# Weight splits ranked 400 instructions earlier, and the second head pair of a gated linear attention projected beside head 1 instead of head 0

## The chip, the cores and the metric

The kernel runs on one core of a Trainium2 chip. The metric is device time in microseconds (us) of one execution. The engines are TensorE (PE in the profile; PEld is its weight load), VectorE (DVE), ScalarE (ACT), GpSimd (POOL) and SyncE (SP), which starts most of the transfers.

## What is computed

512 tokens of width 1024, and 256 context tokens, go through two blocks of two layers each, all in float32. The change acts in the first block. A layer projects the normalised tokens to all inputs of three branches and three gates, and merges the branches:

```python
hx = rms_norm(xs, norm_g) * (1 + scale_x[:, None]) + shift_x[:, None]
px = split_cols(hx @ w_in + b_in)
...
ya_x = conv_module(*px[0:3], dw_w, dw_b, ln_g, ln_b, w_conv_out)
yb_x, yb_c = gla_branch(px[3:9], pc[3:9], gla_w_gate, gla_b_gate, gla_norm_g, w_gla_out, need_ctx)
yc_x, yc_c = attn_branch(px[9:13], pc[9:13], q_norm_g, k_norm_g, w_attn_out, need_ctx)
...
return (jax.nn.sigmoid(p[13]) * ya + jax.nn.sigmoid(p[14]) * yb
        + jax.nn.sigmoid(p[15]) * yc) @ w_out
```

The branch in question is the gated linear attention (GLA): four heads with keys of 64 and values of 128, scanned forward and backward in chunks of 64 tokens, the context first. Per chunk, with `cum` the running sum of the log gate:

```python
q_in = q * jnp.exp(cum)
k_in = k * jnp.exp(-cum)
att = jnp.where(mask, jnp.einsum('bnihd,bnjhd->bnhij', q_in, k_in), 0.0)
o_intra = jnp.einsum('bnhij,bnjhe->bnihe', att, v)
k_state = k * jnp.exp(last[:, :, None] - cum)
contrib = jnp.einsum('bnjhd,bnjhe->bnhde', k_state, v)
...
return dec[..., None] * s + con, s
```

The first layer needs the context's outputs too (768 tokens), the second only those of the 512. The second block (mLSTM and retention) is not touched by name, but uses the same function for its weights.

## The kernel before

All large products are made from pairs: each float32 operand is split into a rounded high part and the rest, and `mm3` (L317) issues three products, high with high, high with low and low with high. Weights come from HBM in granules of 128x1024 or 128x512: `raw` (L270, a transfer started by SP) brings one into a buffer wr, and `split` makes wh from it (L285, ScalarE, a rounded copy) and wl (L286, VectorE, the difference). wr, wh and wl have two buffers each, so that a granule can be split when TensorE has finished with the last but one.

The program is written in Python generators that are woven into each other. What each engine then does in which order is set by a scheduler: of the instructions that are ready by its model, it takes the one with the best rank, and the rank is the order of issue in the program. `high_priority(offset=400)` ranks what is issued under it as if it had come 400 instructions sooner.

In the first block the projections use PSUM tiles `pp` (three banks of 512 columns), and the GLA heads tiles `pm`. The generators of GLA:

- `gla_in`: values, and the queries and keys of heads 0 and 1 through `gla_qk(0)`.
- `gla_qk(hp)`: the queries (here Q1 for hp 1) and then the keys (K1) of heads 2hp and 2hp+1. After each projection the pieces in `pp` are emptied by ScalarE, each half of a piece twice (L935, L936), into tiles bq0 or bk0 for the even head, which have one buffer, and bq1 or bk1 for the odd head, which have two. In layer 0 such a projection is 768 columns, two `pp` tiles of 512 and 256.
- `gla_gate(hd)`: the log gate of a head from L948 on, its running sums (two scans, L956 and L958), the scaled queries and keys (L972, L977, L978), and the keys transposed on TensorE (L984).
- `gla_body(hd, go)`: contributions (L998), 22 state updates (L1008), the masked scores (L1019, L1021, L1025), the head's outputs (L1029, L1033, which reads bq), and their norm (`per_token`, L625 to L641, `rsqrt` L302 to L308, L1040, L1041).
- `gla_`: drives them, with a generator `ahead` that is advanced between the steps of a head's body.

`gla_` is woven with `merge`, which projects the merge gates (granules M00 to M07, copied from PSUM by L763, used by L775) and the conv branch's output (w_conv_out 0 to 7). These products don't depend on GLA and fill TensorE beside it. Attention follows: per two query tiles the scores (L1234), softmax (reduce L1237, exponential L1239, L1240, scaling L1241), transposes (L1254) and the products with the values (L1264), woven with the later gates and the output projections.

Of the kernel before, what the change touches and what calls it, by code (L numbers as in the profile page):

```python
# [9 lines left out]
F32 = mybir.dt.float32  # L10
# [4 lines left out]
AF = mybir.ActivationFunctionType  # L15
ALU = mybir.AluOpType
# [243 lines left out]
class _K:  # L260
# [12 lines left out]
    def split(self, spec, spare=None):  # L273

        nk, nc_ = spec[3], spec[5]
        n = nk * nc_
        r = self.raw(spec)[:, :n]
        if spare is None:
            hi = self.wh.tile([P, 1024], F32R, tag="wh", name="wh")[:, :n]
            lo = self.wh.tile([P, 1024], F32R, tag="wl", name="wl")[:, :n]  # L280
        else:
            c = slice(TX + P * spare, TX + P * spare + n // KT)
            hi, lo = self.hh[:, :, c], self.hl[:, :, c]
            r = r.rearrange("p (k c) -> p k c", k=KT)
        self.nc.scalar.activation(hi, r, AF.Copy)  # L285
        self.nc.vector.tensor_tensor(out=lo, in0=r, in1=hi.bitcast(F32), op=ALU.subtract)  # L286
        return hi, lo

    @staticmethod
# [282 lines left out]
def _chain(*gens):  # L572
    for g in gens:
        yield from g


def _first_block(K, ctx, resp):
# [10 lines left out]
    def layer(l, res, t3p, ctx2, pend):  # L588
        need = l < DEPTH - 1
# [20 lines left out]
        def vec(name, i=0, p0=0, p1=P, half=False):  # L610
            c = _S1[name] + i - (h0 if half else g0)
            return (smh if half else sm)[p0:p1, c:c + 1]
# [115 lines left out]
        def tin(c, segs):  # L728
            return K.proj_t(("w_in", l, 0, 8, c, 128), h, segs)
# [151 lines left out]
        with tc.tile_pool(name="gla", bufs=1) as gp, tc.tile_pool(name="glaps", bufs=8 - K.pp_banks, space=PSUM) as pm:  # L881
# [45 lines left out]
            def gla_qk(hp):  # L927
                for name, col, segs in (("bq", C_Q, outs), ("bk", C_K, full)):
                    pcs = tin(col + 128 * hp, segs)
                    for i in range(2):  # L930
                        t = gp.tile([P, 768], F32, tag=f"{name}{i}", name=name, bufs=1 + i)
                        b_ = vec(name, 2 * hp + i, 64 * i, 64 * i + 64)
                        for ps, s, e in pcs:
                            src = ps[64 * i:64 * i + 64, :]
                            S.activation(t[0:64, s:e], src, AF.Identity, bias=b_)  # L935
                            S.activation(t[64:128, s:e], src, AF.Identity, bias=b_)  # L936
                        qk[name, 2 * hp + i] = t
                    yield
# [118 lines left out]
            def gla_():  # L1057

                yield from gla_gate(0)
                for hd in range(4):  # L1060
                    ahead = _chain(gla_gate(1), gla_qk(1)) if hd == 0 else gla_gate(hd + 1) if hd < 3 else iter(())
                    for i, _ in enumerate(gla_body(hd, go)):
                        if i % 2 == 0 or not need or hd == 0:
                            next(ahead, None)
                        yield
                    for _ in ahead:
                        pass
            gla = gla_()
            n_gla, n0 = (43, 3) if need else (27, 3)
            n_tap = 37 if need else 34  # L1070
# [735 lines left out]
```

## Time and profile before

| | |
|---|---|
| median of 3 runs (range) | 2748.11 us (2747.8 to 2751.84) |
| the profiled execution | 2749.59 us |
| its span | 2747.5 us |
| mean granted TensorE clock | 0.977 of full |
| TensorE busy | 2609.0 us, 95% |
| VectorE busy | 1984.6 us, 72% |
| ScalarE busy | 1089.8 us, 40% |
| chain that ended last, by engine | PE 79%, DVE 15%, ACT 3% |

The trace has one row for each instruction, with its engine, source line, output and input. "Idle before <- releaser" is the time that the engine stood ahead of it, and whose end released it. A wait for several things is put down to the last. PEclk is the TensorE clock that was granted, as a share of 2.4 GHz; its lower level is 1.2 GHz. The first block ends at about 1600 us; layer 0 of it has its GLA heads at about 220 to 370 us, layer 1 at about 1085 to 1235.

### The profile page before, as it was taken

The page shows a single profiled execution, that of the slowest core. Times are in us where ns is not written, and L with a number is a line of the kernel's source. Part 1 is how long each engine was busy: PE and PEld are TensorE (multiplying, and loading weights), DVE is VectorE, ACT ScalarE, POOL GpSimd, SP SyncE. Part 2 cuts the span into 40 slices and gives each one's busy share as a digit, 9 for nine tenths or more (in the row PEclk, how much of TensorE's full clock was granted, in tenths as well). Part 3 has the DMA queues.
Part 4 walks back from the last instruction along what each step waited for, and adds up shares of the span by engine and source line. Part 5 has one row for each costly group of instructions (what it writes and reads, how often), then busy time and mean ns, then how long its engine had stood idle before and what let it go on. Part 6 is the DMA issues. An engine that isn't in the chain of part 4 may idle for free.

```text
span 2747.5 us, 37004 instructions
## 1 busy us (share of the span) xinstructions
PE 2609.0 (95%) x14484; PEld 2222.0 (81%) x14484; DVE 1984.6 (72%) x3691; ACT 1089.8 (40%) x1819; POOL 27.8 (1%) x94
## 2 busy tenths in 40 slices
PE   5998899999899999699999989999999999999998
PEld 3887778888788788578877878888888978888887
DVE  5998565677875599766888678776677678655665
ACT  3234423454532334534545344442333444432332
POOL 0000000000000000000000000000000000000000
PEclk9999999999999999899999999999999999999999
DMA  5210103101253231013134424334332222223222
GB/s 210 64 56 29 39 28 103 55 30 62 71 156 100 88 97 62 27 61 112 58 111 130 139 80 137 121 117 130 123 123 77 82 82 83 84 80 92 77 85 77
DMA packets 78110, 243.18 MB, mean 89 GB/s; under 512 B 9968, under 2 KB 16496, under 8 KB 77808
## 3 DMA queue, kind: packets, MB, share of 16 engines
q1 hardware_dynamic: 72448, 233.37, 27.2%
q10 hardware_dynamic: 5488, 7.44, 0.9%
q8 instruction: 114, 1.87, 0.3%
q14 instruction: 60, 0.49, 0.1%
HBM read 238.68 MB, written 2.10 MB: 88 GB/s over the span
## 4 chain that ended last, share of the span: by engine, by line
PE 79%; DVE 15%; ACT 3%; issue 2%; DMA 1%; ACTq 0%; POOL 0%; DVEq 0%
PE pp L317 63%; PE pm L317 5%; DVE ca L814 4%; PE ov L1264 2%; DVE wl L286 2%; PE sc L1234 2%; DVE SP L1008 2%; PE tr L1254 2%; ACT wh L285 1%; PE pm L1033 1%; PE pm L635 1%; PE pm L625 1%; DVE t L958 1%; PE pm L1685 1%; DVE t L956 0%
## 5 line engine op out<-in xcount | busy, mean ns | idle before, releaser
L317 PE MATMUL pp<-hh,wh 128*128 128x512 f32 (+1 forms) x2080 | 772.5, 373 | 35.1 <-ACT bk L936 12.4
L317 PE MATMUL pp<-hh,wl 128*128 128x512 f32 (+1 forms) x2080 | 768.0, 372 | 28.8 <-DVE wl L286 28.7
L317 PE MATMUL pp<-hl,wh 128*128 128x512 f32 (+1 forms) x2080 | 767.9, 371 | 1.4 <-DVE hl L472 1.3
L285 ACT ACTIVATE wh<-wr 128x1024 fp32r<-128x1024 f32 (+1 forms) x348 | 347.6, 1000 | 769.1 <-PE pp L317 696.8
L286 DVE TENSOR_TENSOR wl<-wr,wh 128x1024 fp32r<-128x1024 f32 (+1 forms) x348 | 399.2, 1148 | 195.5 <-ACT wh L285 190.4
L317 PEld LDWEIGHTS pp<-hh,wh 128*128 128x128 f32 x2080 | 396.6, 191 | 103.2 <-ACT bk L936 13.1
L317 PEld LDWEIGHTS pp<-hh,wl 128*128 128x128 f32 x2080 | 396.4, 191 | 100.7 <-DVE wl L286 36.4
L317 PEld LDWEIGHTS pp<-hl,wh 128*128 128x128 f32 x2080 | 396.9, 191 | 64.8 <-DVE hl L472 3.4
L317 PE MATMUL pp<-wl,hh 128*128 128x256 f32 (+1 forms) x704 | 227.8, 324 | 3.4 <-DVE wl L286 3.2
L317 PE MATMUL pp<-wh,hh 128*128 128x256 f32 (+1 forms) x704 | 225.1, 323 | 3.2 <-ACT u L1572 2.7
L317 PE MATMUL pp<-wh,hl 128*128 128x256 f32 (+1 forms) x704 | 226.3, 322 | 0.0
L814 DVE SCALAR_TENSOR_TENSOR ca<-u,sm,ca 128x783 f32<-128x783 f32 (+1 forms) x240 | 201.7, 890 | 1.1
L317 PEld LDWEIGHTS pp<-wl,hh 128*128 128x128 f32 x704 | 133.8, 190 | 17.0 <-DVE wl L286 7.0
L317 PEld LDWEIGHTS pp<-wh,hh 128*128 128x128 f32 x704 | 133.2, 190 | 15.6 <-ACT u L1572 3.5
L317 PEld LDWEIGHTS pp<-wh,hl 128*128 128x128 f32 x704 | 133.8, 190 | 10.1
L417 DVE CUSTOM_DVE_ANT_0 junk<-mw,cond,bmod 128x1024 bf16<-128x1024 f32 x104 | 132.8, 1277 | 3.4 <-DMA mw<-modw 3.1
L317 PE MATMUL pp<-bh,wh 128*128 128x512 f32 (+1 forms) x288 | 105.6, 368 | 7.2 <-DVE merged L775 3.0
L317 PE MATMUL pp<-bl,wh 128*128 128x512 f32 (+1 forms) x288 | 103.4, 360 | 0.0
L317 PE MATMUL pp<-bh,wl 128*128 128x512 f32 (+1 forms) x288 | 103.2, 361 | 0.0
L317 PE MATMUL pp<-yh,wh 128*128 128x512 f32 (+1 forms) x256 | 93.9, 368 | 0.0
L317 PE MATMUL pp<-yh,wl 128*128 128x512 f32 (+1 forms) x256 | 93.5, 366 | 0.0
L317 PE MATMUL pp<-yl,wh 128*128 128x512 f32 (+1 forms) x256 | 93.4, 366 | 0.0
(377 smaller groups left out, 4266.6 us busy)
## 6 DMA issues: line engine op xcount, KB each, us to landing
wr<-wpack SPq DMA_DIRECT2D x308, 512.0 KB, 3.5
mw<-modw SPq DMA_DIRECT2D x80, 512.0 KB, 3.6
wr<-wpack SPq DMA_DIRECT2D x48, 256.0 KB, 2.7
m<-wpack SPq DMA_DIRECT2D x16, 512.0 KB, 8.2
cond<-cond ACTq DMA_DIRECT2D x5, 512.0 KB, 4.0
res<-xT SPq DMA_DIRECT2D x4, 512.0 KB, 4.9
tf<-xT SPq DMA_DIRECT2D x8, 256.0 KB, 2.6
out<-t SPq DMA_DIRECT2D x16, 128.0 KB, 1.8
```

The lines of the kernel that those rows point to most:

```text
L285: self.nc.scalar.activation(hi, r, AF.Copy)
L286: self.nc.vector.tensor_tensor(out=lo, in0=r, in1=hi.bitcast(F32), op=ALU.subtract)
L317: mm(o, lhsT=lhs[a], rhs=r[b], start=first and p == 0, stop=last and p == 2)
L417: pin(V.tensor_tensor_reduce(out=junk, in0=w, in1=self.cond[:, v, :], scale=1.0, scalar=bias[:, j:j + 1], op0=ALU.mult, op1=ALU.add, accum ...
L625: T.matmul(p1[:, i:i + 1], lhsT=x[:, o:o + P], rhs=ones[:, 0:1], start=True, stop=True)
L635: T.matmul(p2[:, o:o + P], lhsT=r[:, i:i + 1].to_broadcast([P, P]), rhs=ident, start=True, stop=True)
L814: V.scalar_tensor_tensor(out=ca[:, c, :], in0=x, scalar=w, in1=ca[:, c, :], op0=ALU.mult, op1=ALU.add)
L958: V.tensor_tensor_scan(out=cum[64:128, ::-1], data0=reset[64:128, ::-1], data1=ls[64:128, ::-1], initial=0.0, op0=ALU.mult, op1=ALU.add)
L1008: V.scalar_tensor_tensor(out=SP[r, n_, :], in0=SP[r, c_, :], scalar=dec[r, c_:c_ + 1], in1=con[c_][r, :], op0=ALU.mult, op1=ALU.add)
L1234: T.matmul(sc[:, s - k0:e - k0], lhsT=qT[:, t * P:t * P + P], rhs=kT[pi][:, s:e], start=pi == 0, stop=pi == 1)
L1254: T.transpose(tr[:, jj * 256 + q * P:jj * 256 + q * P + P], pr[q][:, (j + jj) * P:(j + jj + 1) * P], ident)
L1264: T.matmul(ov, lhsT=vhl[:, kts[j0 + jj], g].rearrange("p a b -> p (a b)"), rhs=x_[:, jj * 256:jj * 256 + 256], start=j0 + jj + pi == 0, st ...
```

## The change

Two edits. The two instructions of a split are issued under `high_priority(offset=400)`, all through the kernel; the transfer in `raw` is not. And in `gla_` the generator that runs beside the heads' bodies is made up differently: before, head 0 had the gate of head 1 and then the projections Q1 and K1, one step at each of its own; now head 0 has the gate of head 1 alone, and head 1 has Q1, K1 and then the gate of head 2. No instruction is added or removed on any engine; one line is inserted at L285, so that in the changed kernel L285 is L286 and so on.

```diff
--- before.py
+++ after.py
@@ -282,8 +282,9 @@
             c = slice(TX + P * spare, TX + P * spare + n // KT)
             hi, lo = self.hh[:, :, c], self.hl[:, :, c]
             r = r.rearrange("p (k c) -> p k c", k=KT)
-        self.nc.scalar.activation(hi, r, AF.Copy)
-        self.nc.vector.tensor_tensor(out=lo, in0=r, in1=hi.bitcast(F32), op=ALU.subtract)
+        with self.tc.high_priority(offset=400):
+            self.nc.scalar.activation(hi, r, AF.Copy)
+            self.nc.vector.tensor_tensor(out=lo, in0=r, in1=hi.bitcast(F32), op=ALU.subtract)
         return hi, lo
 
     @staticmethod
@@ -1058,9 +1059,9 @@
 
                 yield from gla_gate(0)
                 for hd in range(4):
-                    ahead = _chain(gla_gate(1), gla_qk(1)) if hd == 0 else gla_gate(hd + 1) if hd < 3 else iter(())
+                    ahead = _chain(gla_qk(1), gla_gate(2)) if hd == 1 else gla_gate(hd + 1) if hd < 3 else iter(())
                     for i, _ in enumerate(gla_body(hd, go)):
-                        if i % 2 == 0 or not need or hd == 0:
+                        if i % 2 == 0 or not need or hd == 1:
                             next(ahead, None)
                         yield
                     for _ in ahead:
```

The order of ScalarE in layer 0, from the copies of K1 (bk) to those of Q1's first (bq), before. L985 copies a head's transposed keys, L1036 and L1040 belong to the norm of head 0, L763 to the merge gates:

```order
L935 ACTIVATE bk<-pp,sm 64x256
L936 ACTIVATE bk<-pp,sm 64x256
L935 ACTIVATE bk<-pp,sm 64x256
L936 ACTIVATE bk<-pp,sm 64x256
L985 ACTIVATE kn<-pm 128x256
L985 ACTIVATE kn<-pm 128x512
L1036 ACTIVATE t_2112<-pm 128x256
L763 ACTIVATE merged<-pp,smh 128x512
L1040 ACTIVATE t_2300<-pm 128x256
L285 ACTIVATE wh<-wr 128x1024
L763 ACTIVATE merged<-pp,smh 128x256
L935 ACTIVATE bq<-pp,sm 64x512
```

and of the change (L764 is L763, L286 is L285, L936 and L937 are L935 and L936, L986 is L985, L1037 and L1041 are L1036 and L1040, L966 to L976 are part of the gate of head 1):

```order
L764 ACTIVATE merged<-pp,smh 128x256
L286 ACTIVATE wh<-wr 128x1024
L764 ACTIVATE merged<-pp,smh 128x512
L966 ACTIVATE dec<-last 128x12
L972 ACTIVATE t_2061<-t_2050 128x768
L970 ACTIVATE t_2058<-t_2058 128x768
L1037 ACTIVATE t_2097<-pm 128x256
L976 ACTIVATE t_2050<-t_2050 128x768
L986 ACTIVATE kn<-pm 128x256
L986 ACTIVATE kn<-pm 128x512
L1041 ACTIVATE t_2168<-pm 128x256
L936 ACTIVATE bk<-pp,sm 64x512
```

The copies of the merge gates now stand ahead of those of the keys and queries, and the first copies of bk behind the whole first part of head 0. (The tile's 768 columns come as 512 and 256.)

The order of VectorE in layer 1, beside head 0, before. L956 to L978 are the gate of head 1, L1021 and L1025 the masked scores of head 0; the two wl are the granules M00 (128x1024) and w_conv_out 4 (128x512):

```order
L958 SCALAR_TENSOR_TENSOR t_9779<-reset,t_9743 64x768
L962 COPY last<-t_9779 64x12
L1021 COPY_PREDICATED at_8530<-masks,pm 128x512
L963 COPY last<-t_9779 64x12
L1021 COPY_PREDICATED at_8531<-masks,pm 128x512
L967 TENSOR_TENSOR t_9787<-last,t_9779 128x768
L972 SCALAR_TENSOR_TENSOR bq<-bq,t_9790 128x512
L1025 TENSOR_TENSOR t_9837<-at_8530,at_8531 128x512
L286 TENSOR_TENSOR wl<-wr,wh 128x1024
L977 TENSOR_TENSOR kin<-bk,t_9779 128x512
L286 TENSOR_TENSOR wl<-wr,wh 128x512
L978 TENSOR_TENSOR bk<-bk,t_9787 128x768
```

and of the change, where M00's wl stands about 30 rows further up (ahead of L862) and w_conv_out 4's here, ahead of the last nine state updates:

```order
L1009 SCALAR_TENSOR_TENSOR SP<-SP,dec,pm 64x128 x6
L954 TENSOR_TENSOR t_9743<-t_9743,t_9742 128x768
L287 TENSOR_TENSOR wl<-wr,wh 128x512
L1009 SCALAR_TENSOR_TENSOR SP<-SP,dec,pm 64x128 x9
L957 SCALAR_TENSOR_TENSOR t_9779<-reset,t_9743 64x768
```

```order
L1022 COPY_PREDICATED at_8531<-masks,pm 128x512
L968 TENSOR_TENSOR t_9787<-last,t_9779 128x768
L973 SCALAR_TENSOR_TENSOR bq<-bq,t_9790 128x512
L1026 TENSOR_TENSOR t_9837<-at_8530,at_8531 128x512
L978 TENSOR_TENSOR kin<-bk,t_9779 128x512
L979 TENSOR_TENSOR bk<-bk,t_9787 128x768
L287 TENSOR_TENSOR wl<-wr,wh 128x1024
```

Both splits have left the place among the masked scores; the last row is M01's, which before stood about 30 rows on, in the gate of head 2.

The order of VectorE in the attention of layer 1, before (L1237 to L1241 are the softmax of one tile each, L775 and L778 the merge):

```order
L1237 TENSOR_REDUCE st<-sc 128x1
L1240 RECIPROCAL st<-st 128x1
L1241 TENSOR_SCALAR t_12400<-t_12400,st 128x768
L1237 TENSOR_REDUCE st<-sc 128x1
L286 TENSOR_TENSOR wl<-wr,wh 128x512
L1240 RECIPROCAL st<-st 128x1
L1241 TENSOR_SCALAR t_12411<-t_12411,st 128x768
L1237 TENSOR_REDUCE st<-sc 128x1
L775 SCALAR_TENSOR_TENSOR tf<-tf,pp 128x512
L286 TENSOR_TENSOR wl<-wr,wh 128x1024
L1240 RECIPROCAL st<-st 128x1
```

and of the change:

```order
L1238 TENSOR_REDUCE st<-sc 128x1
L287 TENSOR_TENSOR wl<-wr,wh 128x1024
L1241 RECIPROCAL st<-st 128x1
L776 SCALAR_TENSOR_TENSOR tf<-tf,pp 128x512
L1242 TENSOR_SCALAR t_12400<-t_12400,st 128x768
L1238 TENSOR_REDUCE st<-sc 128x1
L287 TENSOR_TENSOR wl<-wr,wh 128x1024
L1241 RECIPROCAL st<-st 128x1
L779 TENSOR_TENSOR merged<-merged,tf 128x512
L1242 TENSOR_SCALAR t_12411<-t_12411,st 128x768
L1238 TENSOR_REDUCE st<-sc 128x1
```

A split of 128x1024 now follows each of the first two reductions, where there was one of 128x512 in the second.

## Rows read from the trace of the kernel before

**Rows 1.** The page, part 1: busy us, share of the span, instructions.
```profile
PE 2609.0 (95%) x14484; PEld 2222.0 (81%) x14484; DVE 1984.6 (72%) x3691; ACT 1089.8 (40%) x1819; POOL 27.8 (1%) x94
```

**Rows 2.** Waits of TensorE, whole span: total us, times, longest.
```profile
PE pp L317 <- DVE wl L286: 31.9, 19, 9.7
...
PE pp L317 <- ACT bk L936: 12.4, 2, 7.3
```

**Rows 3.** Busy time by windows: window, us, busy us per engine, granted clock.
```profile
220.00:330.00 110.00, 92.02 (x539) 78.85 (x539) 77.86 (x159) 55.09 (x81) 0.00 (x0) 0.89 0.11 34
740.00:765.00 25.00, 18.92 (x88) 15.01 (x87) 19.36 (x30) 8.93 (x15) 0.00 (x0) 0.80 0.40 125
1085.00:1240.00 155.00, 126.03 (x713) 102.67 (x713) 113.20 (x249) 70.15 (x105) 0.00 (x0) 0.88 0.17 52
1380.00:1500.00 120.00, 114.68 (x602) 93.49 (x602) 98.11 (x178) 65.14 (x116) 0.00 (x0) 0.99 0.35 110
```

**Rows 4.** Timeline of ScalarE, layer 0: start us, us, line, [idle before <-releaser].
```profile
297.87 0.68 ACT L935 ACTIVATE bq<-pp,sm 64x512 f32<-64x512 f32 x1 [1.32 <-PE pm L1033]
...
302.10 0.47 ACT L936 ACTIVATE bq<-pp,sm 64x256 f32<-64x256 f32 x1
```

**Rows 5.** Timeline of TensorE, layer 0.
```profile
266.75 0.58 PE L317 MATMUL pp<-hh,wh 128*128 128x256 f32 x1 [5.08 <-ACT bk L936]
...
279.49 0.80 PE L317 MATMUL pp<-hh,wh 128*128 128x512 f32 x1 [7.34 <-ACT bk L936]
280.09 0.63 PE L317 MATMUL pp<-hl,wh 128*128 128x512 f32 x1
...
285.62 0.39 PE L317 MATMUL pp<-hh,wl 128*128 128x512 f32 x1
285.85 0.39 PE L317 MATMUL pp<-hh,wh 128*128 128x512 f32 x1
```

**Rows 6.** Waits of TensorE, 1085 to 1240.
```profile
PE pp L317 <- DVE wl L286: 20.1, 3, 9.7
PE pm L984 <- DVE bk L978: 3.3, 2, 1.9
...
PE pm L1029 <- DVE t L1025: 1.6, 1, 1.6
```

**Rows 7.** Timeline of VectorE, layer 1.
```profile
1129.49 1.22 DVE L286 TENSOR_TENSOR wl<-wr,wh 128x1024 fp32r<-128x1024 f32 x1
...
1131.83 0.96 DVE L978 TENSOR_TENSOR bk<-bk,t 128x768 f32<-128x768 f32 x1
...
1162.14 1.22 DVE L286 TENSOR_TENSOR wl<-wr,wh 128x1024 fp32r<-128x1024 f32 x1
1163.27 0.96 DVE L978 TENSOR_TENSOR bk<-bk,t 128x768 f32<-128x768 f32 x1
```

**Rows 8.** Timeline of TensorE, layer 1.
```profile
1121.12 0.50 PE L317 MATMUL pp<-bh,wh 128*128 128x512 f32 x1 [2.03 <-ACT merged L763]
...
1130.77 0.80 PE L317 MATMUL pp<-hh,wl 128*128 128x512 f32 x1 [8.91 <-DVE wl L286]
...
1163.41 0.79 PE L317 MATMUL pp<-hh,wl 128*128 128x512 f32 x1 [9.72 <-DVE wl L286]
```

**Rows 9.** Waits of ScalarE, whole span.
```profile
ACT wh L285 <- DMA wr<-wpack: 1.7, 2, 1.0
```

**Rows 10.** Waits of TensorE, 1380 to 1500.
```profile
PE pp L317 <- DVE wl L286: 2.9, 2, 2.0
PE pp L317 <- ACT wh L285: 2.3, 2, 1.5
```

**Rows 11.** Line L286 alone by windows: window, us, VectorE's busy us (instructions).
```profile
640.00:765.00 125.00, 10.59 (x10) 0.96 0.21 64
1380.00:1500.00 120.00, 15.00 (x15) 0.99 0.35 110
```

**Rows 12.** Waits of ScalarE, 1380 to 1500.
```profile
ACT wh L285 <- PE pp L317: 17.2, 8, 6.2
```

## The prediction

> **What bounds the kernel now.** I read the page's busy times first: TensorE is busy 2609.0 us, 95% of a span of 2747.5 [rows 1]. The change adds and removes no instruction on any engine, so TensorE's work stays, and all that an order can give back is its idle time (138 us in all) and the time that its products take longer at the lower clock. The waits say who ended that idle time [rows 2]: wl, VectorE's half of a weight split, 31.9 us in 19 waits; bk, the copies of GLA's keys out of PSUM, 12.4 in two. The windows then say where [rows 3]. Two stretches stand out, the GLA heads of layer 0 (220 to 330: TensorE busy 92.0 of 110 us, granted clock 0.89) and of layer 1 (1085 to 1240: 126.0 of 155, 0.88); two smaller ones are the attention tails (740 to 765, and 1380 to 1500). The change moves little elsewhere; the second block, from 1605 us on, I put at nothing.
>
> **Layer 0: the projection of the second pair.** Q1 and K1 (queries and keys of heads 2 and 3) are now issued inside head 0, Q1 first. Its products are done by about 254 us, but eight ScalarE copies must empty its two PSUM banks, and they only run from 297.87 to 302.57, released by L1033, the last product of head 0 that reads bq0 [rows 4]: bq0 has a single buffer, so head 2's queries can't be written before head 0 has done with its own. Of the three banks of the projections two are thus shut for 45 us. K1 and the gate product M05 squeeze through the third, and TensorE stands 5.08 and 7.34 us until K1's copies free it [rows 5]. Both stops also cost clock: from 266.75 to the second stop at 272.15 and from 279.49 to about 285.6 the products run at the lower level (a 512-wide one shows as 0.63 us there, as 0.39 right after), 11.5 us that at full clock would be half: 5.7 us lost.
> After the change, head 0 runs beside the gate products M04, M05 and M06, whose copies (L763) wait for nobody, and Q1 and K1 follow at the end of head 0 and in head 1, when bq0 is almost free. Both stops go: 12.4 + 5.7 = 18 us. What is late next: the norm of head 0 (L625) and the products L1029, which have less independent work before them; the nearest rows are single waits of 1.6 (L1029 on L1025, in layer 1 [rows 6]), and I charge two of them, 3 us (bounds 0 and 8: every head's). Q1's copies now stand directly behind L1033 of head 0, so a bank may still be held for some us; at worst the 7.34 stays. **Layer 0: 15 us less** (bounds 6 and 22).
>
> **Layer 1: the splits of the fill work.** Of the 29 us idle in 1085 to 1240, 20.1 are three waits for wl, 3.3 for bk of L978, 1.6 for L1025 [rows 6]. The two long ones are one pattern [rows 7, 8]. VectorE is busy without a gap with states, scans and masks of two heads, and the split of the next gate weights stands in its list behind them; it runs at 1129.49 and 1162.14, 1.22 us each, and TensorE's product starts right behind it after 8.91 and 9.72 us idle. Ranked 400 instructions earlier, the first goes to before the chain L862 to L876, and the second into the norm of head 0, so the 24 products that hang on each are at hand when the hole opens. SP's loads of the weights follow the new order of the granules and change places with a few loads for the modulation; POOL's list is unchanged; I cost both at nothing: a split waited for its load 1.7 us in two waits of the whole run [rows 9]. But the very next row decides what the hole is worth: L978 (bk), which feeds the transposes L984, ends 1132.79 and 1164.23, 0.9 us behind the split. In head 0 the transposes of head 1 still stand next, and by the two orders there are 38 products instead of 23 between L1019 and L984: 15 more, 3.4 us at the 0.23 us between two starts [rows 5]. So of 8.91, and 2.03 and a little more ahead of it [rows 8], about 9 remain, with L978 as the new name. In head 1 the transposes move behind the norm and M02, w_conv_out 6 and M03 fill: 9.72 falls to about 2. That fill is then missing in head 2, where I expect 8.5 in place of the third wait for wl (1.5) and one for bk of 1.9, and 2 in head 3, where attention's first products fill. With one more of smaller gaps that is 22.5 of the 29.0: 6.5 less. Clock: a mean of 0.88 over 155 us is 37 us at the lower level; some 16 of them lie in the two long holes, 21 are busy, and half of these, 10.6, are lost. One long hole fewer gives back half of its 9.6 us, and the new one in head 2 takes half of that again: 2.4. **Layer 1: 9 us less** (bounds 2, if each hole only changes name; 25, if 20.1 of idle and half the clock loss go). The added wait on L978 holds L984, L1029 and L1033 of that head behind it, as the wait for wl did.
>
> **The tails.** From 740 to 765 TensorE is idle 6.1 us at clock 0.80 [rows 3]; the products of layer 0's last gates come there with their splits made earlier: 4 less (bounds 0 and 7). From 1380 to 1500 the waits for wl and wh are 2.9 and 2.3 [rows 10]: 5 less (bounds 1 and 7, with the clock behind them). At about 1490 a block of products has by then been used up, so some 3 us lie open that were covered: 3 more (bounds 0 and 6).
> **New holds.** In the two attention stretches the splits jump ahead of softmax rows, on ScalarE and on VectorE. There are 10 and 15, 10.6 and 15.0 us of VectorE [rows 11]. A split that is listed early but whose buffer is not yet free also holds what is behind it: from 1380 to 1500 ScalarE stood 17.2 us at splits in eight waits, until TensorE had used up the weights before [rows 12]. I charge 5 us for all of it (bounds 0 and 46: 25.6 of VectorE, 17.2 of ScalarE and an estimated 3 for ScalarE in the first tail), near the lower end, since TensorE is idle only 5.3 of 120 us there [rows 3] of which only 5.2 belong to splits.
> The Trainium skill (PSUM — Partial Sum Buffer, Engine vs sequencer instructions) calls the queues of ScalarE and VectorE strictly first in, first out. By that rule everything listed behind an early split waits with it, ready or not, and the charge would go toward its upper end, at which the sum is 16 us more instead of 25 less; the rows show ScalarE standing, not whether anything behind was ready.
>
> **Sum.** 15 + 9 + 4 + 5 - 3 - 5 = 25 us less, against the profiled execution's 2749.59 (span 2747.5 and 2.1 around it): 2724.6. The median of the three runs is 1.5 below that execution, so 2723 us.
>
> **Rivals.**
> A. The waits only change their name: in layer 1 L978 takes over from wl at full length, in layer 0 Q1's copies hold two banks as long as before, later. For: 0.9 us between split and L978 [rows 7]. Against: the gate products no longer need the held banks. It gives 3 to 8 less, 2743 us. Chance 0.20, of which 0.13 within 0.2% (5.5 us, about what a measurement of this kernel can tell from no change).
> B. Slower: the splits among the softmax rows. In the two attention stretches VectorE's 25.6 and ScalarE's 20 us stand ahead of the reduce, exponential and scaling (L1237 to L1241) that the transposes L1254 and the products L1264 wait for. The forecast has 30 us less without the 5 charged; it is even when 30 of these 46 reach the path, two thirds of it. At four fifths, 37, plus a 3 us hole at the end of the tail, the time is 2749.6 + 10 - 1.5 = 2758. For: VectorE is busy 98 of 120 us there. Against: TensorE's 5.3 us of idle. Chance 0.14. The rule of strict queues named above, taken by itself, leads here.
> C. Both GLA stretches fill nearly whole. Idle 18.0 + 29.0, and clock 8.6 (0.89 over 110 us is 24 at the lower level, some 7 of them idle) + 10.6 us, are 66 us; three quarters of it with the tails even is 50: 2698 us. Against: L978 stays where it was on VectorE. Chance 0.12.
> D. The change doesn't do what it says: the buffers of weights (two) and not their rank set when a split runs. Then only layer 1's splits, which do wait in line, run sooner, and nothing else moves: within 0.2%. Chance 0.02, since TensorE's list itself changes.
>
> **The numbers.** The forecast has 0.52. Faster: 0.52 + 0.12 + 0.07 = 0.71; within 0.2%: 0.13 + 0.02 = 0.15; slower: 0.14. The range, 2701 to 2751, reaches down to both GLA stretches at their upper bounds with the rest even (22 + 25 = 47 less) and up past A and D; it leaves out B and much of C.
>
> **What would show it.** Right: the 12.4 for bk L936 is gone from the waits and the window 220 to 330 is some 15 us shorter for the same products; wl falls from 31.9 to under 15; L984 on L978 rises from 3.3 to 15 or more. Wrong: a wait for bq or bk of 5 us or more in head 1 of layer 0; L1254 or L1264 waiting more than 10 us for VectorE in the attention stretches; or a second block that is not the same within 2 us.

## The result and the profile after

The changed kernel takes 2717.57 us (median of 4 runs, 2715.65 to 2721.02) against 2749.47 of the kernel before on the same chip: a ratio of 0.988, 95% interval 0.9868 to 0.9892, or 32 us less. The forecast was 2723 us with a range of 2701 to 2751; its sign and size hold, and several of its mechanisms do not.

The profiled execution has a span of 2713.9 us, 33.6 below that of before. TensorE's line of the page, part 1, against [rows 1]:

```profile
PE 2599.2 (96%) x14484; PEld 2216.3 (82%) x14484; DVE 1985.8 (73%) x3691; ACT 1090.2 (40%) x1819; POOL 27.6 (1%) x94
```

The same 14484 products are 2599.2 us busy instead of 2609.0. The products are the same, and the mean granted clock rose from 0.977 to 0.986, so I read these 9.8 us as clock: products that ran at the higher level instead of the lower. Idle time fell from 138.5 to 114.7 (span less busy): 23.8 us. Together 33.6.

To see where, I cut both spans at the first residual addition of layer 0's end, at the last of the first block, and at the end. In each piece the kernels do nearly the same instructions (4985, 3777 and 5724 matmul records), so that lengths may be compared, and length less busy time is TensorE's idle time. The windows, before (us, busy us and records of PE, PEld, DVE, ACT, POOL; granted clock, DMA share, GB/s), with the GLA stretch of each layer behind them:

```profile
0.00:876.50 876.50, 806.61 (x4985) 698.04 (x4986) 649.02 (x1152) 350.18 (x597) 3.10 (x18) 0.97 0.24 77
876.50:1594.90 718.40, 673.92 (x3777) 568.78 (x3776) 543.22 (x989) 311.19 (x496) 2.51 (x11) 0.97 0.29 89
1594.90:2747.50 1152.60, 1128.49 (x5724) 955.21 (x5724) 792.32 (x1551) 428.43 (x728) 22.22 (x65) 0.99 0.31 97
223.50:429.30 205.80, 182.95 (x1146) 156.34 (x1146) 137.42 (x327) 81.87 (x125) 0.00 (x0) 0.92 0.13 41
1087.00:1238.30 151.30, 123.69 (x696) 100.50 (x695) 109.91 (x246) 68.69 (x104) 0.00 (x0) 0.88 0.16 49
```

and after:

```profile
0.00:856.80 856.80, 800.65 (x4985) 693.50 (x4986) 648.91 (x1152) 351.20 (x596) 3.10 (x18) 0.98 0.25 78
856.80:1558.80 702.00, 667.75 (x3778) 566.15 (x3776) 544.07 (x989) 310.17 (x496) 2.51 (x11) 0.98 0.29 91
1558.80:2713.90 1155.10, 1130.83 (x5724) 956.68 (x5724) 792.79 (x1552) 428.79 (x728) 21.95 (x65) 0.99 0.32 97
225.80:417.80 192.00, 182.84 (x1169) 154.68 (x1168) 136.67 (x328) 84.32 (x126) 0.00 (x0) 0.98 0.15 45
1068.00:1212.00 144.00, 124.17 (x763) 103.77 (x762) 110.48 (x247) 66.64 (x102) 0.00 (x0) 0.96 0.17 54
```

| | length | idle | busy |
|---|---|---|---|
| layer 0 | -19.7 | 69.9 to 56.2: -13.7 | -6.0 |
| layer 1 | -16.4 | 44.5 to 34.3: -10.2 | -6.2 |
| second block | +2.5 | 24.1 to 24.3: +0.2 | +2.3 |

(Layer 0's GLA heads last until 429 us in the trace of before, not until 370 as the text ahead of the prediction has it; the windows here take them whole.) In the GLA stretches idle time went from 22.9 to 9.2 us and from 27.6 to 19.8, and the granted clock from 0.92 to 0.98 and from 0.88 to 0.96. What a length of a piece is worth: the same program run twice (the version of e4 and e10 below) takes 851.4 and 854.8 us for layer 0, and 703.6 and 698.0 for layer 1, so a difference of 3 to 6 us in a piece of one execution says nothing by itself. The changed kernel, run again (e9), takes 854.9, 703.5 and 1154.3.

From 220 to 330 us, the first window of [rows 3], TensorE now starts 611 products instead of 539 and is granted 0.97 instead of 0.89.

TensorE's waits after, five of the largest, to be read against [rows 2, 6] (one line number further, L287 for L286):

```profile
PE pp L318 <- DVE merged L776: 7.1, 1, 7.1
PE pp L318 <- ACT tf L741: 5.7, 2, 4.8
PE pp L318 <- DVE wl L287: 5.6, 9, 1.4
PE pm L985 <- DVE bk L979: 4.9, 3, 2.6
PE pp L318 <- ACT bk L937: 4.7, 1, 4.7
```

The 31.9 us of waits for wl are 5.6, with none above 1.4; the two waits for bk of layer 0 are gone. New are one of 7.1 for the merge's VectorE step (L776), one of 4.7 for bk in layer 1, 4.8 at the end of layer 0's attention (L741), and 3.9 at the end of layer 1's (L746, not in these lines). L985 for bk of L979, which I had expected at 15 or more, stands at 4.9. The two largest of layer 1 in TensorE's timeline, with one for L979 between them:

```profile
1101.57 0.79 PE L318 MATMUL pp<-hh,wh 128*128 128x512 f32 x1 [4.74 <-ACT bk L937]
...
1112.85 0.88 PE L985 MATMUL pm<-identr,bk 128*128 128x128 f32 x6 [2.56 <-DVE bk L979]
...
1177.16 0.77 PE L318 MATMUL pp<-bh,wh 128*128 128x512 f32 x1 [7.11 <-DVE merged L776]
1177.72 0.63 PE L318 MATMUL pp<-bl,wh 128*128 128x512 f32 x1
```

and VectorE's rows that ended the one of 7.11:

```profile
1174.53 0.68 DVE L287 TENSOR_TENSOR wl<-wr,wh 128x512 fp32r<-128x512 f32 x1
...
1176.34 0.68 DVE L776 SCALAR_TENSOR_TENSOR merged<-merged,pp 128x512 f32<-128x512 f32 x1
1176.93 0.95 DVE L979 TENSOR_TENSOR bk<-bk,t 128x768 f32<-128x768 f32 x1
```

All three PSUM banks of the projections were full (three such steps, L776, follow within 3 us), and the step that empties one stood in VectorE's list behind the scans and masks, where the splits had stood before. Splits stand ahead of it now: two of 0.68 us each, the one shown and one at 1171.53, run while TensorE waits.

### The profile page after: what moved, and what is told of

Its sections match the earlier page's. It is cut to its first block, busy times and chain, and to the rows that moved or that the text cites. A ratio compares the mean times of both kernels' runs of the same rounds, so it can differ in the third digit from the quotient of the medians.

```text
span 2713.9 us, 37040 instructions
## 1 busy us (share of the span) xinstructions
PE 2599.2 (96%) x14484; PEld 2216.3 (82%) x14484; DVE 1985.8 (73%) x3691; ACT 1090.2 (40%) x1819; POOL 27.6 (1%) x94
## 3 DMA queue, kind: packets, MB, share of 16 engines
q1 hardware_dynamic: 72448, 233.37, 27.6%
## 4 chain that ended last, share of the span: by engine, by line
PE 80%; DVE 14%; ACT 3%; issue 2%; DMA 1%; POOL 0%; SPq 0%; ACTq 0%; DVEq 0%
PE pp L318 65%; PE pm L318 5%; DVE ca L815 4%; PE ov L1265 2%; DVE wl L287 2%; PE sc L1235 2%; PE tr L1255 2%; DVE SP L1009 2%; ACT wh L286 1%; DMA m<-wpack 1%; PE pm L1034 1%; PE pm L1686 1%; DVE t L959 1%; PE pm L636 1%; PE pm L626 0%
## 5 line engine op out<-in xcount | busy, mean ns | idle before, releaser
L318 PE MATMUL pp<-hh,wh 128*128 128x512 f32 (+1 forms) x2080 | 771.2, 373 | 27.6 <-ACT hh L472 9.4
L286 ACT ACTIVATE wh<-wr 128x1024 fp32r<-128x1024 f32 (+1 forms) x348 | 347.8, 1000 | 746.4 <-PE pp L318 683.5
L287 DVE TENSOR_TENSOR wl<-wr,wh 128x1024 fp32r<-128x1024 f32 (+1 forms) x348 | 399.3, 1148 | 188.0 <-ACT wh L286 185.2
L318 PEld LDWEIGHTS pp<-wh,hl 128*128 128x128 f32 x704 | 133.8, 190 | 10.2
```

What stands on the lines that cost most here:

```text
L318: mm(o, lhsT=lhs[a], rhs=r[b], start=first and p == 0, stop=last and p == 2)
```

## The experiments

In each run below, the ratio is that to the kernel before on the same chip. The theory at this point: the later projection frees PSUM banks in layer 0, the rank brings the fill of layer 1 (the products that keep TensorE busy beside the heads), and each works in its own layer. The rivals: the rank does it all; or the edits need each other.

### One edit at a time

e1 keeps the old generator and has the rank:

```diff
+        with self.tc.high_priority(offset=400):
             self.nc.scalar.activation(hi, r, AF.Copy)
```

> The kernel before with the rank of the splits alone. Theory (the two edits work in different places: the rank in layer 1 and in the tails, the later projection in layer 0): layer 0's two waits for bk of 5 and 7 us stay, layer 1's waits for wl of 8.9 and 9.7 us go; 10 to 18 us less than before, about 2735. Rival (the rank alone does nearly all, as weights split sooner also fill layer 0's stops): over 26 us less, 2723 or below, and no wait for bk above 3 us between 220 and 330. Second rival (the generator matters in both layers): under 6 us less.

Measured: 2729.72 us (4 runs, 2726.13 to 2733.3), ratio 0.9926 (0.9909 to 0.9942): 20.5 us less, between the theory and the first rival. The waits for bk in layer 0 stay, as 4.1 and 3.0 us; the long ones for wl in layer 1 go (the longest left there is 3.2), but in their place stands one of 8.6 for the merge's step L776, as in the changed kernel. So that wait comes with the rank (before, the longest for this step is 2.0, and in e2 2.5). Windows of layer 0, layer 1 and layer 1's GLA stretch:

```profile
0.00:866.10 866.10, 800.64 (x4985) 693.18 (x4986) 650.76 (x1152) 350.57 (x597) 3.10 (x18) 0.97 0.23 78
866.10:1575.50 709.40, 676.98 (x3777) 575.54 (x3776) 543.43 (x989) 310.93 (x496) 2.51 (x11) 0.97 0.28 90
1077.00:1232.00 155.00, 136.71 (x789) 116.92 (x788) 110.79 (x249) 66.90 (x102) 0.00 (x0) 0.89 0.16 50
```

e2 has the new generator and no rank:

```diff
+                    ahead = _chain(gla_qk(1), gla_gate(2)) if hd == 1 else gla_gate(hd + 1) if hd < 3 else iter(())
+                        if i % 2 == 0 or not need or hd == 1:
```

> The kernel before with the later projection of Q1 and K1 alone. Theory: the 12.4 us of waits for bk go, the first layer ends some 14 to 18 us sooner, and the waits for wl of 8.9 and 9.7 us in layer 1 stay within 3 us; about 2733. Rival (the gain is the rank's): 2745 or more. Second rival (the parts need each other): the two gains of this run and of the rank alone add up to under 26 us of the 32.

Measured: 2747.46 us (10 runs, 2741.59 to 2750.46), ratio 0.9987 (0.9977 to 0.9997): 2.8 us less. Both rivals hold; of the theory, the waits for bk go and those for wl stay, but layer 0 ends 10 us sooner instead of 14 to 18, and the whole gains 3. The same windows, and the waits of layer 1's stretch:

```profile
0.00:866.40 866.40, 806.48 (x4984) 696.90 (x4985) 647.88 (x1152) 350.24 (x596) 3.10 (x18) 0.97 0.24 77
866.40:1591.00 724.60, 681.12 (x3778) 575.04 (x3776) 542.98 (x990) 310.94 (x496) 2.51 (x11) 0.96 0.28 88
1077.00:1235.00 158.00, 130.77 (x696) 106.52 (x695) 109.80 (x246) 67.74 (x103) 0.00 (x0) 0.84 0.16 48
```

```profile
PE pp L318 <- DVE wl L287: 18.8, 4, 9.4
PE pp L318 <- ACT wh L286: 4.7, 1, 4.7
```

Piece by piece, as changes of length (idle, busy) against before:

| | layer 0 | layer 1 |
|---|---|---|
| rank alone | -10.4 (-4.4, -6.0) | -9.0 (-12.1, +3.1) |
| generator alone | -10.1 (-10.0, -0.1) | +6.2 (-1.0, +7.2) |
| both | -19.7 (-13.7, -6.0) | -16.4 (-10.2, -6.2) |

So the theory that each edit works in its own layer falls. In layer 0 both edits help, 10 us each, and the sum is the whole. The rank's part there is not in the attention's end: with it alone the heads of layer 0 end at 421.4 us instead of 429.3, after as many products, which is 7.9 of its 10.4. In layer 1 the generator alone is a loss, the rank alone gives 9, and both give 16: the parts need each other there, and the runs' 20.5 and 2.8 us do not make 32. The idle time does add up (-12.1 and -1.0 against -10.2); what does not is TensorE's busy time, +3.1 and +7.2 against -6.2. I read that as the clock: in the GLA stretch of layer 1 it was granted 0.88 before, 0.89 with the rank, 0.84 with the generator and 0.96 with both. For both edits this repeats (0.95 or 0.96 in e9, e4, e10 and e6, with layer 1 busy 3.5 to 7.8 us less than before); each edit alone has one trace. With the rank alone the stop of 8.6 us is followed by the lower level, 0.50 from 1197 to 1207; with both, the 10 us behind that of 7.1, 1178 to 1188, were granted 0.89. Why so much less is lost behind the second is not settled.

### Were the PSUM banks held by the single buffer?

e3 gives bq0 a second buffer in the kernel before and leaves the order alone. Room is made by a shorter reset pattern, with each running sum in two pieces:

```diff
-                        t = gp.tile([P, 768], F32, tag=f"{name}{i}", name=name, bufs=1 + i)
+                        t = gp.tile([P, 768], F32, tag=f"{name}{i}", name=name, bufs=2 if name == "bq" else 1 + i)
-            reset = gp.tile([P, 768], BF16, name="reset")
+            reset = gp.tile([P, 512], BF16, name="reset")
```

> The kernel before with a second buffer for bq0 and bq1 alike, so that Q1's copies need not wait for head 0's last product; Q1 and K1 stay in head 0. (To make room the reset pattern of the running sums is 512 long and each sum is made in two pieces, 8 more instructions of VectorE in each layer, under 2 us in all.) Theory (the single buffer shut two of three PSUM banks for 45 us): Q1's copies run before 265 us, the waits for bk of 5.08 and 7.34 us go, layer 0 ends 10 to 18 us sooner, about 2735. Rival (TensorE stood there because gates and projections are short of fill, whoever holds the banks): the idle time between 220 and 330 stays above 14 of its 18 us, 2746 to 2750.

Measured: 2750.75 us (10 runs, 2748.06 to 2754.02), ratio 1.0004 (0.9995 to 1.0014). The theory falls; 16.2 of the 18 us of idle time between 220 and 330 are still there, as the rival had it. ScalarE's copies of Q1, and TensorE's stops:

```profile
262.18 0.69 ACT L935 ACTIVATE bq<-pp,sm 64x512 f32<-64x512 f32 x1
...
265.94 0.68 ACT L936 ACTIVATE bq<-pp,sm 64x512 f32<-64x512 f32 x1
...
269.49 0.47 ACT L936 ACTIVATE bq<-pp,sm 64x256 f32<-64x256 f32 x1
```

```profile
269.03 0.58 PE L317 MATMUL pp<-hh,wh 128*128 128x256 f32 x1 [5.27 <-ACT bq L936]
...
280.45 0.80 PE L317 MATMUL pp<-hh,wl 128*128 128x512 f32 x1 [5.62 <-DVE wl L286]
```

The copies no longer wait for L1033 at 297, but they run only from 262 to 270. ScalarE works without a pause from 249 to 276, and until 266 mostly on the conv branch's normalisation (L868 to L872) and the gate of head 1 (L949 to L952), which are listed ahead of them. TensorE stands 5.27 us for them instead of 5.08 for K1's, and then 5.62 for a split.

e8 takes that hold away as well, with those copies ranked 400 earlier:

```diff
+                            with tc.high_priority(offset=400):
                                 S.activation(t[0:64, s:e], src, AF.Identity, bias=b_)
                                 S.activation(t[64:128, s:e], src, AF.Identity, bias=b_)
```

> The kernel before with two buffers for bq0 (the run with the split running sums, which was no faster) and the ScalarE copies of queries and keys ranked 400 earlier, so that neither the buffer nor ScalarE's list holds the banks of Q1. Theory (the banks were what stopped TensorE, and ScalarE's list held them where the buffer no longer did): Q1's copies done by 258, no wait for bq or bk above 1 us in 220 to 330, 6 to 12 us less, about 2741. Rival (ScalarE and VectorE are both full from 249 to 283 and whatever is moved up makes something else late): other waits of the same size, 2747 to 2752.

Measured: 2742.26 us (7 runs, 2740.23 to 2744.98), ratio 0.9966 (0.9955 to 0.9977): 9 us less, as the theory had it. Q1's copies run from 249 to 257, no wait for bq or bk is left in 220 to 330, and the window 220 to 330:

```profile
220.00:330.00 110.00, 98.72 (x574) 83.90 (x573) 81.51 (x170) 59.47 (x87) 0.00 (x0) 0.91 0.11 34
```

has 11.3 us of idle time for 18.0 [rows 3]. The two largest waits that remain there are for wh and for the state updates:

```profile
PE pp L317 <- ACT wh L285: 6.5, 3, 3.0
PE pm L1022 <- DVE SP L1011: 2.7, 1, 2.7
```

So banks that were not emptied did stop TensorE, but two things held them one behind the other, the buffer and ScalarE's list, and taking the buffer's hold away gave nothing. The copies ranked alone, with the single buffer, were not run. Layer 0 is 7.5 us shorter in e8's profiled execution, layer 1, whose copies are ranked too, 2.7.

### The rank in the attention

e4 is the changed kernel with the rank off for the splits issued in the two attention stretches:

```diff
-        with self.tc.high_priority(offset=400):
+        with self.tc.high_priority(offset=400) if self.pri else contextlib.nullcontext():
...
+        K.pri = False
         with tc.tile_pool(name="att", bufs=1) as ap, tc.tile_pool(name="attps", bufs=1, space=PSUM) as pa:
...
-        K.bg_rate = 1.3
+        K.bg_rate, K.pri = 1.3, True
         ab_ = []
```

> The changed kernel with the rank left at its old place for the splits issued in the two attention stretches. Theory (there the early splits neither cost nor bring much): within 4 us of the changed kernel, 2714 to 2722. Rival (the forecast's charge of 5 us and more for splits ahead of softmax rows is real): 5 to 10 us faster than the changed kernel, about 2710. Second rival (the tails' gain comes from those splits): 5 to 9 us slower, about 2725, with waits for wl and wh of 5 us back in the tail of layer 1.

Measured: 2710.45 us (4 runs, 2709.59 to 2710.99), ratio 0.9855 (0.9841 to 0.987). The first rival's time holds: the rank costs some 7 us there. e9 and e10 are the changed kernel and e4's program once more, now side by side.

> The changed kernel once more, on the same chip as the next three: 2714 to 2721, to compare them with.

> The run with the rank off in both attentions once more. Theory (the early splits there use up the fill that the end of the attention needs, 4.8 and 3.9 us of idle and the clock behind it): 5 to 9 us below the changed kernel of this call. Rival (the difference of 7 was between chips): within 3 us of it.

The change: 2716.44 us (4 runs, 2714.51 to 2717.31), ratio 0.9877 (0.9863 to 0.989). Without the rank in the attentions: 2709.59 (4 runs, 2706.48 to 2711.83), ratio 0.9853 (0.9838 to 0.9868). The runs do not overlap; the difference is 6.9 us, as before.

Is it softmax that was late, as the charge in the sum had it? TensorE's waits from 640 to 770 us in the changed kernel, all of them:

```profile
PE pp L318 <- ACT tf L741: 4.8, 1, 4.8
PE tr L1255 <- ACT qT L1223: 0.4, 2, 0.2
```

No: transposes and value products (L1255, L1265) hardly wait, there or in the attention of layer 1 (0.6 and 0.2 us from 1271 to 1500). What waits is the projection that follows the attention, 4.8 us for the gated output (L741), and in e4 this is

```profile
PE pp L318 <- ACT tf L741: 1.8, 1, 1.8
```

With earlier splits more of the other products run before the attention's end. In both kernels the last VectorE step of the merge (L779) starts 274 us behind the end of the heads. From there to the end of the addition of the last value product (L1273) it is 47.1 us in the changed kernel, with 298 products on TensorE, and 43.3 us in e4, with 280. Behind it TensorE starts 5 products in the next 4.8 us in the changed kernel, and 21 in 4.4 us in e4. So the attention ends later, and little is left to cover its end. e9 and e10 show the same (299 and 280 products, 47.1 and 43.3 us). The prediction had this as "3 more" at the end of layer 1 alone.

e6 has the rank off in layer 0's attention only (`K.pri = not need` in e4's edit):

> The changed kernel with the rank off in the attention of layer 0 alone; in layer 1's attention it stays. Theory (only layer 0 pays: its fill is used up and the gated output stands 4.8 us open; layer 1 gained some 1 us by its early splits): 2707 to 2711, as fast as with both off or a little faster. Rival (both attentions pay alike): half way, 2713 to 2715.

Measured: 2713.28 us (4 runs, 2711.73 to 2716.56), ratio 0.9864 (0.9847 to 0.9881). That is half way, the rival's time, but the interval overlaps with those of e9 and of e10, so the medians do not decide it. The traces show the price in layer 0: from the end of its heads to its end it is 439.0 and 438.9 us with the rank there (the changed kernel, e9), and 435.5, 435.2 and 435.1 without (e4, e10, e6). For layer 1, whose rank e6 leaves on, they don't: 346.9, 346.0 and 345.8 with the rank, 346.2 and 344.0 without, although e6 has the wait for the gated output at the end of its attention, 1440 to 1500 us, as in the changed kernel, and e4 has none:

```profile
PE pp L318 <- ACT bh L746: 3.9, 1, 3.9
```

e11 leaves the rank on beside the GLA heads and nowhere else:

```diff
+        K.pri = True
         with tc.tile_pool(name="gla", bufs=1) as gp, tc.tile_pool(name="glaps", bufs=8 - K.pp_banks, space=PSUM) as pm:
...
+        K.pri = False
         with tc.tile_pool(name="att", bufs=1) as ap, tc.tile_pool(name="attps", bufs=1, space=PSUM) as pa:
```

> The changed kernel with the rank on in the two GLA stretches alone: off in the attentions, between the layers and in the whole second block. Theory (all that the rank brings it brings beside the GLA heads, and the second block lost 1 to 2 us by it): 2705 to 2711, equal to the run with the rank off in the attentions or up to 4 us below. Rival (the rank also helped between the layers and in the second block): 2712 to 2718.

Measured: 2714.63 us (4 runs, 2713.65 to 2721.4), ratio 0.9877 (0.9863 to 0.989), some 5 us above e10 on the same chip: the rival. (Its profiled execution is the slowest of the four, 2721.4 us, so the trace shows more than these 5.) The stops at the end of layer 0's attention are back one for one as they were before:

```profile
PE ov L1267 <- DVE ao L1275: 2.1, 1, 2.1
PE pp L318 <- ACT tf L741: 1.9, 1, 1.9
PE pp L318 <- DVE wl L287: 1.7, 1, 1.7
```

e4 has the rank off for the splits issued in the attention and on for those of the products that come after it, and lacks these stops. So I take the splits that help there to be the latter, which with the rank reach back into the attention's end: the rank gives there from behind and takes from inside. The second block did lose by it, as expected there: it is 1153.2 us long here, against 1155.1 in the changed kernel; over all executions 1153.8 to 1155.1 with the rank and 1152.6 to 1153.8 without, about 1 us.

### How far the rank must reach

> As the run before, with a rank of 150 instructions instead of 400. Theory (what counts is that the split stands ahead of the state updates and scans of one head, some 50 VectorE rows): within 4 us of the 400. Rival (the split has to pass a whole head and more, with every engine's instructions counted): half of the gain in layer 1 is lost, 5 to 10 us more.

e12 is e11 with `offset=150`. Measured: 2725.98 us (5 runs, 2723.02 to 2732.36), ratio 0.9917 (0.9904 to 0.9929), 11 us above e11: the rival, and a little more than it. In layer 1 (1085 to 1235) a wait for wl of 6.2 us is back:

```profile
PE pp L318 <- DVE wl L287: 9.6, 4, 6.2
PE pp L318 <- ACT merged L764: 4.7, 1, 4.7
```

The rank counts instructions of all engines, and the state updates, scans and masks that a split has to pass are few of them. Where the 11 us lie the traces do not show: e12's is its fastest execution and e11's its slowest, and their spans differ by 1.6 us.

### What is late next, and what the holes cost in clock

e7 adds to e4 a rank for the merge's VectorE step, the 7.1 us wait of the changed kernel:

```diff
+                    with tc.high_priority(offset=400):
                         V.scalar_tensor_tensor(out=th[:, s:e], in0=th[:, s:e], scalar=1.0, in1=ps, op0=ALU.add,
                                                op1=ALU.mult)
```

> As the run with the rank off in both attentions, and the merge's VectorE step that empties a PSUM bank (merged, the wait of 7.1 us in layer 1) ranked 400 earlier as well. Theory (three PSUM banks full and waiting for VectorE are what is late next in layer 1): that wait goes, 4 to 9 us less, 2702 to 2706. Rival (the scaled keys of L978 stand one row behind it on VectorE and take its place): 2708 to 2712, with 5 us or more of waits of L984 for bk.

Measured: 2716.03 us (4 runs, 2712.88 to 2718.71), ratio 0.9872 (0.9854 to 0.9889), some 5 us above e4, which ran on another chip; the intervals overlap, the runs do not: neither. The wait goes, and the keys of L978 take its place only in part (5.1 us in four waits, none above 1.8); the heads end as in e4, and then TensorE stands 8.65 us at the start of the attention, for its keys:

```profile
1233.02 1.33 PE L1194 MATMUL tr<-identr,t 128*128 128x128 f32 x5 [8.65 <-ACT t L1184]
```

What covered that place had been used up: the last merge step before the attention (L776) starts 30.6 us before the end of head 3 here, 22.9 in e4. From the end of the heads to the end of layer 1 it takes 351.6 us, for 346.2 in e4 and 344.0 in e10. I read it as the same giving back as in the attention.

e5 puts products without a use into the two holes of layer 1 in the kernel before, so that TensorE does not stand:

```diff
+        for _ in range(warm):
+            s, e = segs[0]
+            self.nc.tensor.matmul(views[s], lhsT=hi[:, 0:ncol], rhs=h[0][0][:, s:e], start=True, stop=True)
         for s, e in segs:
             for k in range(nk):
```

> The kernel before with 34 products of 512 columns without a use put ahead of each of the granules M00 and M01 of layer 1, into the very PSUM bank that the granule's own first product then starts afresh; they run in the two holes of 8.9 and 9.7 us, 68 products of 0.22 us, 15 us of work in all. Theory (a good half of layer 1's extra gain was clock, lost behind the holes): the granted clock of 1085 to 1240 rises from 0.88 to 0.93 or more, and the time is 3 to 7 us below the kernel before although it does more, 2744 to 2747. Rival (the clock there does not hang on these holes, or the work behind them is not what is late): the clock stays below 0.90 and the time is that of before or up to 8 us above it.

Measured: 2751.02 us (10 runs, 2746.37 to 2756.78), ratio 1.0 (0.9989 to 1.0012).

```profile
1085.00:1240.00 155.00, 140.91 (x759) 115.02 (x759) 111.16 (x247) 68.03 (x104) 0.00 (x0) 0.91 0.15 49
```

```profile
1131.03 0.50 PE L317 MATMUL pp<-hh,wl 128*128 128x512 f32 x1 [3.49 <-DVE wl L286]
1131.36 0.40 PE L317 MATMUL pp<-hh,wh 128*128 128x512 f32 x1
...
1132.71 0.63 PE L317 MATMUL pp<-hh,wl 128*128 128x512 f32 x1
```

The clock rises from 0.88 to 0.91 only, and the lower level still comes, at 1132 us and later, behind what is left of the holes (3.49 us here); the time is that of before. So 15 us of products cost nothing there and bring nothing. A reading that fits is that VectorE's list sets when the heads go on, and a faster product waits for it: the transposes wait 6.3 us for bk there, for 3.3 [rows 6]. The few other products that moved with the added ones leave this run less clean than the others; that the clock alone, without the fill, would be worth anything is not shown.

## Why the prediction was right, and where it was not

**The sum.** 25 us were forecast, 31.9 measured by the medians. Layer 0 (15 and 4 for its tail) measured 19.7 in one execution and 21.6 in the other. Layer 1 with its tail, less the charges (9 + 5 - 3 - 5 = 6), measured 16.4 and 14.9. So the 7 us that the forecast lacks are in layer 1, which gave 10.4 and 8.9 more, while the second block took some back. Of the 10.4, 3.8 are busy time (clock), 1.3 idle time in the heads, and 5.4 idle time outside them, where the sum had 3 us more and 2.4 less were measured. That layer 0's 19 came out is luck: the later projection alone gave 10.1 for its 15, and the rank alone 10.4 for its 4.

**Layer 0, "released by L1033 ... bq0 has a single buffer".** The two stops went as forecast, but the cause named was half of one: e3 took the buffer's hold away and gave nothing, since ScalarE's list held the same copies until 270; e8 took both away and gave 9. And half of layer 0's gain, 10.4 us, comes from the rank (e1), to which the working gave nothing before the tail; 7.9 of them lie before the heads' end.

**Layer 1, idle time.** "6.5 less" was 7.8 (27.6 to 19.8). The name was wrong: L978 did not take over (4.9 us in all, not 15 or more). The fill lasted longer than worked out by the orders, and what it waited for in the end was PSUM, emptied by L776 on VectorE, a wait that the working left out. One reading of a row was off as well: M00's split ends at 1130.71, 2.1 us and not 0.9 ahead of the end of L978; between them stands the split of w_conv_out 4 (0.69 us).

**Layer 1, clock: the term that was mis-sized.** "2.4" stands against 6.2 us less busy time in layer 1 (4.1 in e9). The working took one long hole fewer and a new one; in the changed kernel the holes are 7.1 and 4.7 us and the stretch is granted 0.96, where either edit alone leaves 0.89 or 0.84. So the two edits do not add up in layer 1, and the difference is in the busy time. Why it stays up with both is not settled: e5, with the two long holes of before mostly filled, was granted 0.91.

**"At about 1490 a block of products has by then been used up ... 3 more", and "new holds ... 5".** The sum of 8 was of the right size, by luck: e10 is 6.9 us below the change, but the mechanism of the 5, splits ahead of softmax rows, is not in the trace (L1255 0.4 us, L1265 none from 640 to 770). The mechanism of the 3 is, at the price of 3.7 us in layer 0, where the working had none of it; in layer 1 its wait of 3.9 us is there, and its price is not shown. The rule of the Trainium skill that was set against the 5 (PSUM — Partial Sum Buffer, Engine vs sequencer instructions: ScalarE's and VectorE's queues are first in, first out) is not contradicted by that: TensorE hardly waited there for what was listed behind the splits. No run here shows what a held split costs where something on TensorE's path stands behind it. In e3 the copies stood behind work that ScalarE was doing, not behind an instruction that waited.

**The second block at nothing.** It is 2.5 us longer in one execution and 1.7 in the other; the prediction counted more than 2 as a sign against it. Of its other signs, that L984 on L978 rises to 15 or more did not come; the waits for bk and wl fell as it said.

**The rivals.** A, waits that only change their name, happened in places (8.9 and 9.7 us for wl became 7.1 for L776 and 4.7 for bk; e3) but not in the whole. B did not: its rows held up nothing that TensorE waited for. C would have needed both stretches nearly without idle time; 9.2 and 19.8 us are left. D did not: the rank alone (e1) gave 20.5 us.

## What to carry to other kernels

Look for the next holder before a wait is put down to a buffer: a PSUM bank can be held by the buffer behind it and by the list of the engine that empties it, and here a second buffer showed nothing until the copies moved up as well. Work that fills TensorE beside a slow chain is a fixed stock: ranking it earlier helps where a hole stands open, and can open another where the same products used to cover the end of a stage. Here the kernel takes 2709.6 us instead of 2716.4 when the splits issued in the attentions go without the rank. Two edits that shorten holes in the same stretch can be worth more together than their sum; here the difference was in the busy time of the same products, so read busy time and idle time apart.

## What the hardware did that I had not expected

TensorE's busy time for the same 14484 products ran from 2597.4 us (e10) to 2616.7 (e2), and the kernel with fewer idle microseconds than before (e2: 127.5 for 138.5 in its profiled execution) gave 7.7 of the 11 back in busy time, which I read as clock. And 15 us of products without a use (e5) left the time as it was, within 0.12%.
